# A two-layer encoder on one core: shorter decay chain, middle conv taps on ScalarE, rotary products beside the root, keys and queries transposed later

## The chip, the cores and the metric

The kernel runs on one core of a Trainium2 chip. The metric is the device time of one execution in microseconds, the median of several runs. TensorE (PE) multiplies matrices into PSUM banks, VectorE (DVE), ScalarE (ACT) and GpSimd (POOL) do the elementwise work, SyncE (SP) issues most DMA loads.

## The reference

The input is x (1, 256, 1024). After a LayerNorm, two layers each add a token mixer and a mixture of 32 experts, and normalise again:

```
p = h @ w_in                                   # 1024 -> 5648
ya = attention(rope(rms(aq)), rope(rms(ak)), av)          # 8 heads, 2 kv heads
yb = neighbourhood attention(bq, bk, bv) + rpb            # 4 heads
q, k, v = silu(conv5(cq, ck, cv)); q, k = l2norm(q), l2norm(k)
beta = sigmoid(b); g = -exp(A_log) * softplus(a + dt_bias)
yc = rms(delta_forward + delta_backward) * silu(cz)       # chunks of 64
mix = sig(ga)*(ya @ wa) + sig(gb)*(yb @ wb) + sig(gc)*(yc @ wc)
h = LN(alpha*h + mix @ w_out);  h = LN(alpha*h + moe(h))
```

In the delta rule g is summed within a chunk and exponentiated (the decay), beta weighs the update, and each chunk needs the inverse of a unit triangular 64x64 matrix per head.

## The kernel before

All 256 tokens stand in two tiles of 128 partitions (t = 0, 1). A layer is a mixer (about 0 to 235 us, and 705 to 940) and a MoE stage whose expert weights stream in.

**The mixer's projections** are the main line. The weights come in units in the order of ORDER (ga0, cqk, cz, cv, akv, aq, ga1, bqk, bv, gb, gc), then the branch weights and w_out. For each unit SP loads w, ACT casts the high part uh, and DVE or (indices of POOL) GpSimd subtracts it to get the low part ul (`stream`, L278); PE then makes three products, high by high, low by high, high by low (`mm3`, L192). Loads run four units ahead. Where places of the mixer come free, loads of expert weights are issued between them (`fetch_freed`, L406).

**Side lines** are generators: "delta" (`delta_line`, L625), "key" (L599), "query" (L611) and "attention" (L1013, L1050). `pump` (L339) steps a line between projection matmuls once an estimated PE clock has passed its due time, and LAGS (L47) holds the lag after each yield. So LAGS sets where a side line's PE work stands among the projections. PE's order is the written one (`pinned`); the orders of DVE, ACT, POOL and SP are made by a scheduler from the program and its priorities.

**Delta line.** cz has beta's and the decay's raw inputs in columns 256 to 272. They are copied to ba (L630); from them come beta (tanh) and g, by a series for softplus on 16 columns, ten scalar_tensor_tensor steps (L174 is `stt`, L169 and L171 are `ts` with one and two scalars, L165 is `tt`). g and its two halves feed eb, six small matmuls into a PSUM bank; db spreads g for the pairwise decays E, which POOL and DVE mask and multiply by beta. qk is the transposition to token-major of the convolved q and k (cs0, cs1), followed by a square, a sum and the root (`rsqrt`, L239: DVE scales and adds eps, POOL takes the power -0.5), kh and qd are the normalised products, kT, qdT their transpositions, gr the grams. Out of them comes the inverse: a round trip through DRAM, some thirty small POOL steps, two writes to DRAM, and two loads back on SP (placeC<-d).

**Conv** (L554): per channel half a first tap on DVE (128x256, `ts`) and four more by `stt`.

**Keys and queries** (`norm_rope`, L569): square on ACT, sum and scale on DVE, root on POOL, product with the root on DVE, two rotary products on POOL, product with the cosine and the sum on DVE. kTA and qTA are their transpositions on PE.

**Merge** (L1123): each branch's product is weighted by its gate and summed into mix; `turn_mix` transposes mix (tpm).

In the trace, "placeA" to "placeK" are the mixer's places of SBUF, "gap" a small one (g, ba, beta's and decay's tiles), "sb" and "eb" PSUM banks.

Of the kernel before, what the change touches and what calls it, by code (L numbers as in the profile page):

```python
# [48 lines left out]
    "key": [10.0],  # L49
    "query": [16.22, 1.92, 1.92],  # L50
# [67 lines left out]
def kernel(ctx: ExitStack, tc: tile.TileContext, a: dict, out: bass.AP):  # L118
# [120 lines left out]
    def rsqrt(o, x, scale, eps, n):  # L239

        with tc.high_priority(offset=PRI):
            ts(V, o, x, scale, OP.mult, eps, OP.add)
            return G.tensor_tensor(out=o, in0=o, in1=mhalf[:, :n], op=OP.pow)
# [74 lines left out]
    def mixer(l, fetch, norm):  # L318
# [233 lines left out]
        cs = [of(f"cs{i}", 2, S) for i in range(3)]  # L552

        def conv(i, b):  # L554

            bv = b.rearrange("p (m s) -> p m s", m=2)
            y = of(f"cy{i % 2}", 2, S)
            for m in range(2):
                ch = 2 * i + m
                ts(V, y[:, m], bv[:, m], cw[:, ch, 2:3], OP.mult)  # L560
                for j in (0, 1, 3, 4):
                    s = j - 2
                    t0, t1 = max(0, -s), S - max(0, s)
                    stt(y[:, m, t0:t1], bv[:, m, t0 + s:t1 + s], cw[:, ch, j:j + 1], y[:, m, t0:t1],
                        OP.mult, OP.add)
            A.activation(bv, y, AF.Tanh)
            stt(cs[i], bv, 1.0, y, OP.add, OP.mult)


        def norm_rope(b, t, n, which, dst, name):  # L570
# [3 lines left out]
            xv = x8(x[:, :n * 64])  # L574
            raw = x8(b) if which else xv
            if not which:
                A.copy(x[:, :n * 64], b)
            sq = y
            A.activation(sq[:, :n * 64], b if which else x[:, :n * 64], AF.Square)
            rs = of(f"rs{t}", 8)  # L580
            V.tensor_reduce(out=rs[:, :n], in_=x8(sq[:, :n * 64]), axis=AX.X, op=OP.add)
            rsqrt(rs[:, :n], rs[:, :n], 1.0 / 64.0, 1e-6, n)
            tt(V, xv, raw, rs[:, :n, None].to_broadcast([128, n, 64]), OP.mult)
            yv = x8(y[:, :n * 64])
            s5 = gc_[:, which, 1, t].rearrange("p (a b e) -> p a b e", a=2, b=2)
            for b_ in range(2):
# [38 lines left out]
        def delta_line(vbank, zb):  # L625

            szg = of("szg", 2, 256)
            ba = of("ba", 2, 2, 2, 4)
            for t in range(2):
                V.tensor_copy(ba[:, :, :, t], zb[t][:, 256:272].rearrange("p (a d h) -> p a d h", a=2, d=2))  # L630
                A.activation(szg[:, t], zb[t][:, :256], AF.Tanh, scale=0.5)
                stt(szg[:, t], szg[:, t], 1.0, zb[t][:, :256], OP.add, OP.mult)
            tt(G, szg.rearrange("p t (h d) -> p (t h) d", d=64), szg.rearrange("p t (h d) -> p (t h) d", d=64),
               gn[:, 2:3].to_broadcast([128, 8, 64]), OP.mult)
# [4 lines left out]
            av = ba[:, 1].rearrange("p d t h -> p (d t h)")  # L639
# [3 lines left out]

            def dh(ap8):

                return ap8.rearrange("p (d h) -> p d h", d=2)[:, :, None, :].to_broadcast([128, 2, 2, 4])

            xx, ax, ee, ss, pp, g = (sc[:, i] for i in range(6))

            sb = bank("s", f"sb{l}")  # L650
            rr, sq_, acc = (sb[:, 16 * i:16 * i + 16] for i in range(3))
            tt(V, xx.rearrange("p (d t h) -> p d t h", d=2, t=2), ba[:, 1], dh(al[:, 1]), OP.add)
# [5 lines left out]
            tt(V, ss, ee, rr, OP.mult)  # L658
            tt(V, pp, sq_, ss, OP.mult)
# [32 lines left out]
            edl = ev[:, 16:32].rearrange("p (d x) -> p d x", d=2)  # L692
# [25 lines left out]
            for t in range(2):  # L718
# [8 lines left out]
                rsqrt(rk[:, t], rk[:, t], 1.0, 1e-6, 8)  # L727
# [35 lines left out]
            G.tensor_copy(kq[:, 1], cs[0])  # L763
# [359 lines left out]
        def merge(br):  # L1123
# [545 lines left out]
```

## Time and profile before

| what | us |
|---|---|
| median of 3 runs | 1431.82 |
| lowest, highest | 1430.55, 1435.36 |
| profiled execution, own time | 1430.76 |
| its span | 1429.0 |
| mean granted clock of TensorE | 0.986 |

The span is what the views show; the execution's own time is 1.76 us more. A row of a timeline has the start, the duration, the engine and line, the instruction (out<-in) with its shape, and in brackets how long the engine stood idle before it and what released it. Rows of the same instruction in sequence are drawn together (x8). A row of windows gives for a stretch the time that PE was busy and the mean clock granted to it, 1.00 being 2.4 GHz.

### The profile page before, as it was taken

How to read it: one execution, taken by the hardware profiler on the slowest of the kernel's cores; microseconds unless marked ns; L12 is line 12 of the kernel's file. 1: busy time of each engine (PE TensorE's matmuls, PEld its weight loads, DVE VectorE, ACT ScalarE, POOL GpSimd, SP SyncE). 2: the span in 40 equal slices, each digit the busy share in tenths (PEclk: the TensorE clock that was granted, in tenths of full speed). 3: DMA queues.
4: the chain of work that ended last, by engine and by line, in shares of the span. 5: the costliest groups of instructions: out<-in, count | busy, mean ns of one | idle time of the engine just before them, and what ended most of it. 6: DMA issues, size and time to landing. Idle time of an engine off the chain costs nothing. (4 is left out here: it accounts for less than half of the span.)

```text
span 1429.0 us, 23895 instructions
## 1 busy us (share of the span) xinstructions
PE 1347.2 (94%) x9778; PEld 893.0 (62%) x9778; DVE 610.5 (43%) x1221; ACT 400.2 (28%) x761; POOL 257.9 (18%) x327
## 2 busy tenths in 40 slices
PE   8999999899999999999889999999999899999986
PEld 7877787655555555554477877875565555655632
DVE  6887567522221222222368866773222122222214
ACT  4445543221111111111145465332111111111111
POOL 4475303300000000000046661132000000000000
PEclk9989999999999999999999999999999999999998
DMA  7635769899999999999856466798999999999994
GB/s 233 211 118 142 257 235 356 312 407 419 419 419 417 419 419 420 418 419 420 334 154 195 123 195 228 271 352 322 419 419 418 418 419 418 420 419 419 418 419 194
DMA packets 114531, 479.86 MB, mean 336 GB/s; under 512 B 25168, under 2 KB 38000, under 8 KB 65520
## 3 DMA queue, kind: packets, MB, share of 16 engines
q1 hardware_dynamic: 112464, 471.85, 84.6%
q0 software_dynamic: 1376, 5.24, 1.0%
q8 instruction: 79, 1.29, 0.4%
q10 hardware_dynamic: 576, 1.18, 0.2%
q14 instruction: 36, 0.29, 0.1%
HBM read 476.40 MB, written 1.84 MB: 335 GB/s over the span
## 5 line engine op out<-in xcount | busy, mean ns | idle before, releaser
L180 PE MATMUL h<-w,h 128*64 128x256 f32 x2016 | 231.3, 385 | 19.4 <-PEq L1413 9.5
L180 PEld LDWEIGHTS h<-w,h 128*64 128x64 f32 x2016 | 143.5, 138 | 98.1 <-issue 14.9
L174 DVE SCALAR_TENSOR_TENSOR hid<-gate,h 128x256 f32<-128x256 f32 x64 | 26.9, 421 | 395.1 <-ACT gate L1505 395.1
L174 DVE SCALAR_TENSOR_TENSOR op<-mo,rt,op 64x512 fp32r<-64x512 f32 x128 | 96.0, 750 | 221.8 <-ACT op L1536 220.9
L1536 ACT ACTIVATE op<-mo,rt 64x512 fp32r<-64x512 f32 x128 | 87.4, 683 | 311.2 <-PE mo L180 271.7
L180 PE MATMUL mo<-w,hidT 128*64 128x512 f32 x720 | 167.7, 595 | 3.6 <-ACT hidT L1517 1.4
L165 POOL TENSOR_TENSOR W<-P,rt 128x128 f32<-128x128 f32 x64 | 24.2, 398 | 773.2 <-PE PT L186 700.9
L1505 ACT ACTIVATE gate<-h 128x256 f32<-128x256 f32 x64 | 24.5, 383 | 404.3 <-PE h L180 404.3
L180 PEld LDWEIGHTS mo<-w,hidT 128*64 128x64 f32 x720 | 51.3, 137 | 92.2 <-issue 79.3
L180 PE MATMUL h<-w,xg 128*64 128x256 f32 x864 | 96.9, 380 | 2.4 <-ACT h L1479 2.4
L180 PE MATMUL h<-wl,h 128*64 128x256 f32 x768 | 86.3, 381 | 2.2 <-ACT h L1479 1.4
L180 PEld LDWEIGHTS h<-w,xg 128*64 128x64 f32 x864 | 61.0, 137 | 34.3 <-ACT h L1479 3.8
L180 PEld LDWEIGHTS h<-wl,h 128*64 128x64 f32 x768 | 53.9, 137 | 30.6 <-ACT h L1479 2.4
L180 PE MATMUL mo<-wl,hidT 128*64 128x512 f32 x304 | 70.0, 597 | 1.6 <-DMA wl<-in_w_dram 1.5
L180 PE MATMUL my<-op,PT 128*128 128x512 f32 x256 | 69.3, 410 | 0.8 <-DVE op L174 0.6
L180 PEld LDWEIGHTS my<-op,PT 128*128 128x128 f32 x256 | 45.4, 188 | 23.9 <-issue 13.2
L180 PE MATMUL xg<-P,hh 128*128 128x256 f32 x256 | 54.8, 294 | 0.0
L180 PEld LDWEIGHTS xg<-P,hh 128*128 128x128 f32 x256 | 39.1, 188 | 24.5 <-issue 24.2
L180 PE MATMUL h<-wl,xg 128*64 128x256 f32 x416 | 48.3, 382 | 5.5 <-DMA wl<-in_w_dram 3.9
L180 PE MATMUL xg<-P,hl 128*128 128x256 f32 x256 | 51.1, 281 | 0.0
L180 PEld LDWEIGHTS mo<-wl,hidT 128*64 128x64 f32 x304 | 20.6, 137 | 36.5 <-issue 30.1
L180 PEld LDWEIGHTS h<-wl,xg 128*64 128x64 f32 x416 | 28.6, 137 | 23.0 <-DMA wl<-in_w_dram 7.1
(458 smaller groups left out, 2451.1 us busy)
## 6 DMA issues: line engine op xcount, KB each, us to landing
w<-in_w_dram SPq DMA_DIRECT2D x268, 1024.0 KB, 19.9
wl<-in_w_dram SPq DMA_DIRECT2D x112, 1024.0 KB, 19.9
w_gb<-in_w_in_dram SPq DMA_DIRECT2D x16, 512.0 KB, 3.5
w_gc<-in_w_in_dram SPq DMA_DIRECT2D x16, 512.0 KB, 4.5
w_wo<-in_w_out_dram SPq DMA_DIRECT2D x16, 512.0 KB, 4.4
w_ga<-in_w_in_dram SPq DMA_DIRECT2D x14, 512.0 KB, 5.7
w_cqk<-in_w_in_dram SPq DMA_DIRECT2D x8, 512.0 KB, 3.4
w_aq<-in_w_in_dram SPq DMA_DIRECT2D x8, 512.0 KB, 4.8
```

The lines of the kernel that those rows point to most:

```text
L165: return eng.tensor_tensor(out=o, in0=x, in1=y, op=op).ins
L174: return V.scalar_tensor_tensor(out=o, in0=x, scalar=s, in1=y, op0=op0, op1=op1)
L180: ins = T.matmul(o, l, r, start=start, stop=stop, skip_group_check=True).ins
L1505: A.activation(g, b[:, :256], AF.Tanh, scale=0.5)
L1536: A.activation(hi, src, AF.Copy, scale=w)
```

## The change

Seven edits. (1) LAGS: the key line steps 15 instead of 10 after its start, the query line 22.5 instead of 16.22. (2) The middle tap of each conv half is an activation on ACT. (3) cs0 is an alias of kq[:, 1], so the copy L763 goes. (4) In `norm_rope` the rotary and cosine products take the unscaled input, the root is multiplied in last; keys work in place in PSUM; the scale and eps of the roots of keys, queries and qk are on POOL. (5) The decay chain reads cz's bank instead of ba, has -exp(A_log) ready as nea, keeps more operands in PSUM, and writes the two halves of g straight from acc; beta and the szg product come later. (6) A second exponential of eb stays in PSUM and feeds nbe and kds. (7) Branch c's merge writes into its PSUM bank and sums into mix on DVE at high priority.

```diff
-    "key": [10.0],
-    "query": [16.22, 1.92, 1.92],
+    "key": [15.0],
+    "query": [22.5, 1.92, 1.92],
...
-    def rsqrt(o, x, scale, eps, n):
+    def rsqrt(o, x, scale, eps, n, eng=V):
...
-            ts(V, o, x, scale, OP.mult, eps, OP.add)
+            ts(eng, o, x, scale, OP.mult, eps, OP.add)
...
-        cs = [of(f"cs{i}", 2, S) for i in range(3)]
+        cs = [kq[:, 1]] + [of(f"cs{i}", 2, S) for i in (1, 2)]
...
-                ts(V, y[:, m], bv[:, m], cw[:, ch, 2:3], OP.mult)
+                A.activation(y[:, m], bv[:, m], AF.Copy, scale=cw[:, ch, 2:3])
...
-            if not which:
-                A.copy(x[:, :n * 64], b)
-            sq = y
-            A.activation(sq[:, :n * 64], b if which else x[:, :n * 64], AF.Square)
+            A.copy(x[:, :n * 64], b)
+            A.activation(dst, x8(b) if which else xv, AF.Square)
...
-            rsqrt(rs[:, :n], rs[:, :n], 1.0 / 64.0, 1e-6, n)
-            tt(V, xv, raw, rs[:, :n, None].to_broadcast([128, n, 64]), OP.mult)
+            rsqrt(rs[:, :n], rs[:, :n], 1.0 / 64.0, 1e-6, n, G)
...
+            xv = x8(b) if which else xv
             tt(V, xv, xv, gc_[:, which, 0, t:t + 1].to_broadcast([128, n, 64]), OP.mult)
-            tt(V, dst, xv, yv, OP.add)
+            tt(V, xv, xv, yv, OP.add)
+            tt(V, dst, xv, rs[:, :n, None].to_broadcast([128, n, 64]), OP.mult)
...
-            for t in range(2):
-                V.tensor_copy(ba[:, :, :, t], zb[t][:, 256:272].rearrange("p (a d h) -> p a d h", a=2, d=2))
...
-            A.activation(beta, ba[:, 0].rearrange("p d t h -> p d (t h)"), AF.Tanh, scale=0.5)
-            ts(V, beta, beta, 0.5, OP.mult, 0.5, OP.add)
...
+            for t in range(2):
+                tt(V, by_t(xx)[:, :, t], by_d(zb[t][:, 264:272]), by_d(al[:, 1]), OP.add)
+            for t in range(2):
+                A.activation(by_t(th_)[:, :, t], by_d(zb[t][:, 256:264]), AF.Tanh, scale=0.5)
...
-            ts(V, xx, xx, 0.0, OP.max)
-            stt(acc, acc, 2.0, xx, OP.mult, OP.add)
-            tt(V, g.rearrange("p (d t h) -> p d t h", d=2, t=2), acc.rearrange("p (d t h) -> p d t h", d=2, t=2),
-               dh(ea), OP.mult)
-            ts(V, g, g, -1.0, OP.mult)
+            stt(acc, xx, 0.0, acc, OP.max, OP.add)
+            tt(V, g, acc, nea, OP.mult)
+            for c2 in range(2):
+                decayed = stt(sc[:, c2], acc, C("half")[:, c2:c2 + 1], nea, OP.mult, OP.mult).ins
...
+            ts(V, beta, th_, 0.5, OP.mult, 0.5, OP.add)
...
-                ts(V, sc[:, c2], g, C("half")[:, c2:c2 + 1], OP.mult)
...
+            A.activation(eb[:, 64:128], eb[:, :64], AF.Exp)
             A.activation(ev, eb[:, :64], AF.Exp)
...
-                rsqrt(rk[:, t], rk[:, t], 1.0, 1e-6, 8)
+                rsqrt(rk[:, t], rk[:, t], 1.0, 1e-6, 8, G)
...
-            G.tensor_copy(kq[:, 1], cs[0])
...
-                    stt(x, x, 1.0, b, OP.add, OP.mult)
-                    if br != "a":
-                        tt(G if br == "b" or t else V, mix[:, t, sl], mix[:, t, sl], x, OP.add)
+                    if br != "c":
+                        stt(x, x, 1.0, b, OP.add, OP.mult)
+                        if br == "b":
+                            tt(G, mix[:, t, sl], mix[:, t, sl], x, OP.add)
+                    else:
+                        with tc.high_priority(offset=PRI):
+                            stt(b, x, 1.0, b, OP.add, OP.mult)
+                            tt(V, mix[:, t, sl], mix[:, t, sl], b, OP.add)
```

What this moves in the built program stands at three places. The first is DVE at the end of the decay chain, before eb (g and its halves are in gap, the accumulator in sb). Before:

```order
L174 SCALAR_TENSOR_TENSOR sb_606<-sb_606,gap_83 128x16
L190 TENSOR_TENSOR ul_ga_868<-w_ga_767,uh_ga_867 128x1024
L165 TENSOR_TENSOR gap_83<-sb_606,gap_83 128x16
L581 TENSOR_REDUCE placeS_108<-placeH_105 128x2
L169 TENSOR_SCALAR gap_83<-gap_83 128x16
L171 TENSOR_SCALAR placeS_108<-placeS_108 128x2
L169 TENSOR_SCALAR gap_83<-gap_83,placeK_109 128x16 x2
```

And now:

```order
L174 SCALAR_TENSOR_TENSOR sb_596<-sb_596,gap_83 128x16
L174 SCALAR_TENSOR_TENSOR placeA_99<-cv_513,placeS_108,placeA_99 128x254
L174 SCALAR_TENSOR_TENSOR sb_596<-gap_83,sb_596 128x16
L174 SCALAR_TENSOR_TENSOR placeA_99<-cv_513,placeS_108,placeA_99 128x255
L165 TENSOR_TENSOR gap_83<-sb_596,gap_83 128x16
L174 SCALAR_TENSOR_TENSOR gap_83<-sb_596,placeK_109,gap_83 128x16
L190 TENSOR_TENSOR ul_ga_774<-w_ga_711,uh_ga_773 128x1024
L174 SCALAR_TENSOR_TENSOR gap_83<-sb_596,placeK_109,gap_83 128x16
L171 TENSOR_SCALAR placeS_108<-sb_596 128x16
```

What were four instructions for g and its halves are three, without the sign flip; the first cut of ga1 (ul_ga) stands behind g instead of three of them ahead, and the taps of cv (placeA<-cv) are still under way.

The second is PE at the first transposition of the queries, among bqk's products. Before:

```order
L180 MATMUL bqk_982<-placeT_110,ul_bqk_962 128x256
L186 MATMUL qdT_1038<-cst,placeF_103 128x128 x4
L186 MATMUL qdT_1044<-cst,placeF_103 128x128 x4
L186 MATMUL qTA_1050<-cst,placeE_102 128x128 x4
L180 MATMUL bqk_981<-placeT_110,uh_bqk_961 128x256
```

And now:

```order
L180 MATMUL bqk_985<-placeT_110,uh_bqk_988 128x256
L180 MATMUL bqk_985<-placeU_111,uh_bqk_988 128x256
L180 MATMUL bqk_985<-placeT_110,ul_bqk_989 128x256
L180 MATMUL bqk_985<-placeT_110,uh_bqk_988 128x256
L180 MATMUL bqk_985<-placeU_111,uh_bqk_988 128x256
L180 MATMUL bqk_985<-placeT_110,ul_bqk_989 128x256
L186 MATMUL qTA_1177<-cst,placeE_102 128x128 x4
```

qTA stood right behind qdT, inside the second unit of bqk; now twelve products, the sixteen grams and twelve more products lie between. In the same way kTA, which stood between db and the last aq products, now stands behind three products of ga1, and all six last aq products come before the qk transpositions.

The third is POOL behind the decays E (placeF) and DVE at the first unit of bqk. On POOL (placeH<-placeH,placeA is a rotary product, mhalf the power of a root, placeD<-placeA a kd product), before:

```order
L165 TENSOR_TENSOR placeF_103<-placeF_103,placeK_109 128x512
L165 TENSOR_TENSOR placeF_103<-placeF_103,placeS_108 128x512
L243 TENSOR_TENSOR placeS_108<-placeS_108,mhalf 128x8 x3
L165 TENSOR_TENSOR placeH_105<-placeH_105,placeA_99 128x16x16 x2
L243 TENSOR_TENSOR placeS_108<-placeS_108,mhalf 128x8
L165 TENSOR_TENSOR placeH_105<-placeH_105,placeA_99 128x16x16 x2
```

And now:

```order
L165 TENSOR_TENSOR placeH_105<-placeH_105,placeA_99 128x16x16 x2
L165 TENSOR_TENSOR placeF_103<-placeF_103,placeK_109 128x512
L165 TENSOR_TENSOR placeF_103<-placeF_103,placeS_108 128x512
L171 TENSOR_SCALAR placeS_108<-placeS_108 128x8
L243 TENSOR_TENSOR placeS_108<-placeS_108,mhalf 128x8
L171 TENSOR_SCALAR placeS_108<-placeS_108 128x8
L165 TENSOR_TENSOR placeH_105<-placeH_105,placeA_99 128x16x16
L243 TENSOR_TENSOR placeS_108<-placeS_108,mhalf 128x8
L165 TENSOR_TENSOR placeH_105<-placeH_105,placeA_99 128x16x16
L171 TENSOR_SCALAR placeS_108<-placeS_108 128x8
L243 TENSOR_TENSOR placeS_108<-placeS_108,mhalf 128x8
L165 TENSOR_TENSOR placeD_101<-placeA_99,placeS_108 128x512 x2
```

The rotary products of the first query tile stand ahead of the mask and beta products of E, those of the second between the roots, and each root has its TENSOR_SCALAR on POOL. On DVE, at ul_bqk (placeA<-qk is kh, placeF<-qk are qd), before:

```order
L165 TENSOR_TENSOR placeA_99<-qk_835,placeS_108 128x256
L165 TENSOR_TENSOR placeF_103<-qk_835,gap_83 128x256 x2
L190 TENSOR_TENSOR ul_bqk_944<-w_bqk_865,uh_bqk_943 128x1024
L165 TENSOR_TENSOR placeA_99<-qk_847,placeS_108 128x256
L165 TENSOR_TENSOR placeF_103<-qk_847,gap_83 128x256 x2
```

And now:

```order
L165 TENSOR_TENSOR placeA_99<-qk_835,placeS_108 128x256
L165 TENSOR_TENSOR placeF_103<-qk_835,gap_83 128x256 x2
L165 TENSOR_TENSOR placeA_99<-qk_847,placeS_108 128x256
L190 TENSOR_TENSOR ul_bqk_947<-w_bqk_862,uh_bqk_946 128x1024
L165 TENSOR_TENSOR placeF_103<-qk_847,gap_83 128x256 x2
```

ul_bqk has changed places with kh of the second tile. Later, SP issues the first load of gc behind the two loads of the inverse instead of ahead of them; ACT's cast of that unit stands before the exponentials of the third attention step instead of behind them; and six more gb products stand on PE before that step's transposition.

## Rows read from the trace of the kernel before

**Rows 1.** The page, part 1: busy us, share, instructions of PE; PEld, DVE, ACT, POOL.
```profile
PE 1347.2 (94%) x9778; PEld 893.0 (62%) x9778; DVE 610.5 (43%) x1221; ACT 400.2 (28%) x761; POOL 257.9 (18%) x327
```

**Rows 2.** Timeline of PE, both mixers: start, duration, instruction [idle before <-releaser].
```profile
71.02 1.23 PE L180 MATMUL eb<-gap,placeK 128*128 128x8 f32 x8 [3.14 <-DVE gap L169]
...
101.17 0.44 PE L186 MATMUL qTA<-cst,placeE 128*128 128x128 f32 x2 [2.73 <-DVE placeE L165]
...
121.14 0.33 PE L186 MATMUL pT_a<-cst,placeH 128*128 128x128 f32 x1 [0.59 <-DVE placeH L169]
...
775.06 2.74 PE L180 MATMUL eb<-gap,placeK 128*128 128x8 f32 x12 [3.38 <-DVE gap L169]
...
806.03 0.69 PE L186 MATMUL qTA<-cst,placeE 128*128 128x128 f32 x2 [3.52 <-DVE placeE L165]
```

**Rows 3.** Windows of PE: stretch, us, PE busy, granted clock, DMA share, GB/s.
```profile
70.00:80.00 10.00, 8.98 (x29) 0.66 0.44 135
100.00:110.00 10.00, 8.83 (x84) 0.83 0.54 173
770.00:785.00 15.00, 11.62 (x44) 0.77 0.48 150
805.00:815.00 10.00, 8.97 (x87) 0.83 0.52 164
```

**Rows 4.** Timeline of DVE in the first mixer.
```profile
53.03 0.47 DVE L169 TENSOR_SCALAR placeA<-cv,placeS 128x256 f32<-128x256 f32 x1
...
61.98 0.16 DVE L169 TENSOR_SCALAR sb<-gap 128x16 f32<-128x16 f32 x1
...
62.35 1.23 DVE L171 TENSOR_SCALAR placeS<-placeS 128x2 f32<-128x2 f32 x1
...
64.92 1.21 DVE L190 TENSOR_TENSOR ul_ga<-w_ga,uh_ga 128x1024 fp32r<-128x1024 f32 x1
...
109.72 1.31 DVE L190 TENSOR_TENSOR ul_bv<-w_bv,uh_bv 128x512 fp32r<-128x512 f32 x1 [0.94 <-ACT uh_bv L190]
```

**Rows 5.** Timeline of ACT in the first mixer.
```profile
82.75 0.60 ACT L577 COPY placeH<-aq 128x512 f32<-128x512 f32 x1
...
139.12 0.47 ACT L992 ACTIVATE placeH<-s_a,placeS 128x256 f32<-128x256 f32 x1 [2.15 <-PE o_a L180]
...
145.06 1.05 ACT L190 CAST uh_gc<-w_gc 128x1024 fp32r<-128x1024 f32 x1 [2.81 <-DMA w_gc<-in_w_in_dram]
```

**Rows 6.** Timeline of POOL, first mixer and (last row) second.
```profile
27.52 0.31 POOL L169 TENSOR_SCALAR placeS<-placeS 128x30 f32<-128x30 f32 x1 [6.53 <-DMA placeS<-in_conv_w_dram]
...
80.19 1.79 POOL L165 TENSOR_TENSOR placeF<-placeF,placeK 128x512 f32<-128x512 f32 x1 [2.40 <-DVE placeF L165]
82.06 1.04 POOL L165 TENSOR_TENSOR placeF<-placeF,placeS 128x512 f32<-128x512 f32 x1
83.21 5.48 POOL L243 TENSOR_TENSOR placeS<-placeS,mhalf 128x8 f32<-128x8 f32 x3
89.56 2.42 POOL L165 TENSOR_TENSOR placeH<-placeH,placeA 128x256 f32<-128x256 f32 x2 [0.87 <-DVE placeH L165]
...
787.06 6.47 POOL L243 TENSOR_TENSOR placeS<-placeS,mhalf 128x8 f32<-128x8 f32 x3
```

**Rows 7.** Timeline of PE, first mixer, from the first qk transposition on.
```profile
79.58 0.38 PE L186 MATMUL qk<-cst,placeB 128*128 128x128 f32 x2
...
80.38 0.48 PE L180 MATMUL aq<-uh_aq,placeT 128*128 128x512 f32 x1
...
81.15 0.40 PE L180 MATMUL ga<-uh_ga,placeT 128*128 128x512 f32 x1
...
92.67 0.28 PE L180 MATMUL bqk<-placeU,uh_bqk 128*128 128x256 f32 x1
92.78 0.28 PE L180 MATMUL bqk<-placeT,ul_bqk 128*128 128x256 f32 x1
...
145.87 1.03 PE L186 MATMUL pT_a<-cst,placeH 128*128 128x128 f32 x8
```

More of the change, by code (lines that the diff above doesn't have):

```diff
@@ L573, in norm_rope @@
             x, y = of(f"ring{turn}", 512), of(f"ring{turn + 1}", 512)
-            xv = x8(x[:, :n * 64])
-            raw = x8(b) if which else xv
-            if not which:
-                A.copy(x[:, :n * 64], b)
-            sq = y
-            A.activation(sq[:, :n * 64], b if which else x[:, :n * 64], AF.Square)
+            xv, yv = x8(x[:, :n * 64]), x8(y[:, :n * 64])
+            A.copy(x[:, :n * 64], b)
+            A.activation(dst, x8(b) if which else xv, AF.Square)
             rs = of(f"rs{t}", 8)
-            V.tensor_reduce(out=rs[:, :n], in_=x8(sq[:, :n * 64]), axis=AX.X, op=OP.add)
-            rsqrt(rs[:, :n], rs[:, :n], 1.0 / 64.0, 1e-6, n)
-            tt(V, xv, raw, rs[:, :n, None].to_broadcast([128, n, 64]), OP.mult)
-            yv = x8(y[:, :n * 64])
+            V.tensor_reduce(out=rs[:, :n], in_=dst, axis=AX.X, op=OP.add)
+            rsqrt(rs[:, :n], rs[:, :n], 1.0 / 64.0, 1e-6, n, G)
             s5 = gc_[:, which, 1, t].rearrange("p (a b e) -> p a b e", a=2, b=2)
@@ L627, in delta_line @@
             szg = of("szg", 2, 256)
-            ba = of("ba", 2, 2, 2, 4)
-            for t in range(2):
-                V.tensor_copy(ba[:, :, :, t], zb[t][:, 256:272].rearrange("p (a d h) -> p a d h", a=2, d=2))
[L631 to L634, printed above, removed]
+            sb = bank("s", f"sb{l}")
+            rr, sq_, acc, th_ = (sb[:, 16 * i:16 * i + 16] for i in range(4))
+            by_t = lambda ap: ap.rearrange("p (d t h) -> p d t h", d=2, t=2)
+            by_d = lambda ap: ap.rearrange("p (d h) -> p d h", d=2)
             beta = of("beta", 2, 8)
-            A.activation(beta, ba[:, 0].rearrange("p d t h -> p d (t h)"), AF.Tanh, scale=0.5)
-            ts(V, beta, beta, 0.5, OP.mult, 0.5, OP.add)
             sc = of("gsc", 8, 16)
-            av = ba[:, 1].rearrange("p d t h -> p (d t h)")
+            xx, ax, ee, ss, pp, g = (sc[:, i] for i in range(6))
             ea = of("ea", 8)
@@ L642, in delta_line @@
                 A.activation(ea, al[:, 0], AF.Exp)
[L644 to L652, printed above, removed]
+            nea = sc[:, 6]
+            for t in range(2):
+                ts(G, by_t(nea)[:, :, t], by_d(ea), -1.0, OP.mult)
+            for t in range(2):
+                tt(V, by_t(xx)[:, :, t], by_d(zb[t][:, 264:272]), by_d(al[:, 1]), OP.add)
+            for t in range(2):
+                A.activation(by_t(th_)[:, :, t], by_d(zb[t][:, 256:264]), AF.Tanh, scale=0.5)
+                A.activation(szg[:, t], zb[t][:, :256], AF.Tanh, scale=0.5)
+                stt(szg[:, t], szg[:, t], 1.0, zb[t][:, :256], OP.add, OP.mult)
             stt(ax, xx, -1.0, xx, OP.mult, OP.max)
@@ L657, in delta_line @@
             tt(V, sq_, ee, rr, OP.mult)
-            tt(V, ss, ee, rr, OP.mult)
-            tt(V, pp, sq_, ss, OP.mult)
+            stt(ss, ee, 2.0, rr, OP.mult, OP.mult)
+            stt(pp, sq_, 0.5, ss, OP.mult, OP.mult)
             ts(V, acc, pp, 1.0 / 19.0, OP.mult)
@@ L686, in delta_line @@
             for c2 in range(2):
-                ts(V, sc[:, c2], g, C("half")[:, c2:c2 + 1], OP.mult)
                 mm(eb[:, 32 + c2 * 16:48 + c2 * 16], C("ones"), sc[:, c2], True, True)
             ev = of("ev", 64)
+            A.activation(eb[:, 64:128], eb[:, :64], AF.Exp)
             A.activation(ev, eb[:, :64], AF.Exp)
             egc = ev[:, 0:16].rearrange("p (d x) -> p d x", d=2)
-            edl = ev[:, 16:32].rearrange("p (d x) -> p d x", d=2)
+            egp, edl = (eb[:, 64 + 16 * i:80 + 16 * i].rearrange("p (d x) -> p d x", d=2) for i in range(2))
             egl = ev[:, 32:64].rearrange("p (c d t h) -> p c d t h", c=2, d=2, t=2)
@@ L697, in delta_line @@
                 t, hs = c // 2, slice(c % 2 * 64, c % 2 * 64 + 64)
-                stt(nbe[hs, c], egc[hs, 0, t * 4:t * 4 + 4], -1.0, beta[hs, 0, t * 4:t * 4 + 4], OP.mult, OP.mult)
-                ts(V, nbe[hs, 3 - c], egc[hs, 1, t * 4:t * 4 + 4], -1.0, OP.mult)
+                stt(nbe[hs, c], egp[hs, 0, t * 4:t * 4 + 4], -1.0, beta[hs, 0, t * 4:t * 4 + 4], OP.mult, OP.mult)
+                ts(V, nbe[hs, 3 - c], egp[hs, 1, t * 4:t * 4 + 4], -1.0, OP.mult)
             kds = of("kds", 2, 8)
```

2 lines of the change are left out of this document (added).

## The prediction

> **What bounds the kernel now.** I read the page's busy shares first: TensorE (PE) is busy for 94% of the span [rows 1], so time can be won only where it stands still or runs slowly. PE's order is written out and fixed, so the second view is PE's timeline, for its waits. Each mixer holds two long ones [rows 2]: the decay sums eb wait for DVE, 3.14 us in the first layer and 3.38 in the second, and the queries' transposition qTA waits for DVE's last product, 2.73 and 3.52. Together that is 12.77 us. A short wait stands before the first softmax's transposition, 0.59. Third come the windows: behind each of the four long waits the granted clock falls towards its lower level, 1.2 of 2.4 GHz [rows 3]. A mean of 0.66 over 10 us is a loss of 3.4 us; the other three rows give 1.7, 0.23 x 15 = 3.45, and 1.7. Sum 10.25. So the change can remove 12.77 + 10.25 = **23.0 us**, if both waits vanish and nothing takes their place.
>
> **The change, part by part.**
>
> *The decay wait (conv taps, decay chain, roots).* PE is through with what it has at 71.02 - 3.14 = 67.9 and waits for g. DVE works without a gap ahead of it, so what counts is how much DVE work still stands there. Six taps of 0.47 go to ScalarE [rows 4]: 2.8. A TENSOR_SCALAR that writes SBUF takes 1.23 while POOL works, one that writes PSUM 0.16 [rows 4]; three such held ones go (operands in PSUM, the root's scale on POOL): 3.2. Three ul_ga of 1.21 [rows 4], ahead of g so far, stand behind it now: 3.6. The last taps of cv and the second half of the key's norm go behind it as well. Together 9.6 us, against the 3.1 needed; were half of that wrong, 4.8 would still do. What is late next is ACT (its taps and the key's square), for which some 1.7 us are left. I take the wait and the low clock behind it as gone.
>
> *The queries' wait.* Both qTA now stand behind the grams. The second query root ends on POOL after the third one of the next paragraph: two kd products of at most 1.79 each, a scale and a root of 1.83, together some 5.6 us [rows 6]. PE has 60 bqk matmuls at 0.11 from start to start [rows 7] and 28 smaller ones between there and the first qTA, over 8 us, and DVE's last product of 0.7 fits as well. The wait goes.
>
> *The new wait: bqk's first lo part.* PE cannot pass its third bqk matmul without ul_bqk. On DVE that subtraction used to stand before the second kh product; now it stands behind it, and this product waits for POOL's third root. Ahead of the root POOL has the rotary products, which used to come after. From the last aq matmul I add: query copy 0.60 [rows 5]; rotary pair 2.42; mask product 1.79; beta product 1.04; three roots 5.48; second rotary pair 2.42 [rows 6]; three scales of 128x8, each put at 0.2, between nothing and the 0.31 of one with 30 columns [rows 6], 0.6; kh, by the tap of its size, 0.47 [rows 4]; ul_bqk 1.21, by ul_ga's shape. Sum 16.0. PE over the same stretch: from the first qk transposition to the third bqk matmul 92.78 - 79.58 = 13.20, less 0.77 for three aq (80.38 to 81.15), and with the four key transpositions that now lie in it, at half of the 0.80 that eight of qk take: 12.8 [rows 7]. So PE waits **3.2 us per layer**. Bounds: 1.3 (copy beside the first bank's end, scales free, the mask product at the beta product's 1.04) and 4.5 (the roots at the second layer's 6.47, scales at 0.31). Behind waits of 2.73 to 3.52 the low level cost 1.7 or more [rows 2, 3], and 3.2 lies among these. But PE was at full clock and busy for long before this place, so it may also pass; I charge 1.7 once for the two layers (bounds 0 and 3.4).
>
> The scales on POOL are the place where a rule speaks against the change. The rows have 0.31 us for a scale on POOL and 1.23 for a held one on DVE [rows 4, 6]. The Trainium skill (GPSIMD Engine Reference, 4.1 Engine selection) sends elementwise work to VectorE and calls POOL about twice as slow on two inputs. By that each scale would cost twice DVE's unheld 0.16, and the wait would be 0.4 us longer per layer, an estimate; by the rows DVE is the dearer place as long as POOL holds it up. The sum stands without this.
>
> *The third attention step.* ACT's cast of the first w_gc stood behind that step's exponentials; now it stands before them. SP used to issue that load ahead of the two loads of the inverse, and now issues it behind them. The load that stood behind them before landed at 145.06 [rows 5]. The chain that leads there starts with the grams on DVE, where a wait of 0.94 for a cast [rows 4] need not come again: 144.1. Then a cast of 1.05, four exponentials of 0.47 [rows 5], and three short steps (the o_a cast, two on DVE) at the tap's 0.47: ready at 148.4. PE's transposition stood at 145.87 [rows 7]. Six more gb matmuls stand before it, 1.5 by the three aq, and the 0.59 is gone: 146.8. So it waits 1.6 us (bounds 0, and 2.5 with the 0.94 kept), against 0.59 that goes: net **1.0 per layer**.
>
> *What costs nothing.* The alias of cs0 takes a copy off POOL at a time when POOL then waits for DVE; without that cover it would be a gain. The merge's last sums on DVE spare the tail's transpositions a wait for POOL, and the later transposition of yc gives about as much back. The beta tanh, beta and nea lie beside other work. In the MoE stage the loads start when mixer places come free, so what the mixer gains passes through.
>
> *Sum.* 23.0 - 6.4 - 1.7 - 2.0 = 12.9 us. The profiled execution took 1430.76 (span 1429.0), 1.06 under the median of the three runs shown. 1430.76 - 12.9 = 1417.9; on the median's footing **1418.9**. Its own range by the bounds: 23.0 - 2.6 + 1.2 = 21.6 gained, 1410.2, up to 23.0 - 9.0 - 1.7 - 3.8 = 8.5 gained, 1423.3.
>
> **The rivals.**
>
> *No new wait at bqk.* It needs 3.2 us less ahead of ul_bqk, and the third step as before: all of 23.0 is kept, 1408.8. For it: POOL's spans are rough, and a root that DVE does not hold up may be shorter. Against it: 5.48 and 6.47 for three roots. Chance 0.20.
>
> *All new waits at their upper bounds.* 4.5 + 1.7 + 1.9 per layer, 16.2 in all, so 6.8 are left: 1425.0. For it: the second layer's rows are the longer ones. Chance 0.16.
>
> *Slower: the inverse's loads do not come earlier with PE.* Place: SP holds w_gc behind those loads, ACT stands in its cast before the exponentials, PE waits before the third transposition. If that load lands at 145.06 as before, the transposition is ready at 145.06 + 1.05 + 1.9 + 1.4 = 149.4 instead of 145.87, 3.5 later in each layer whatever was won ahead, and the low level costs 1.7 on top: 1431.8 + 10.4 = 1442.2. It decides once those loads move by less than 3.5 us. Against it: the grams that start the chain come earlier by as much as PE does. Chance 0.07.
>
> *The change does not do what it says.* eb still waits, now for ACT's taps and the key's square, or what the mixer wins is waited for again at the MoE's loads: 1431.8. Against it: 9.6 us of DVE work moved for 3.1 us of wait. Chance 0.07.
>
> **How the numbers follow.** The forecast has 0.50. The range 1408 to 1425 holds it with its bounds, the rival without a wait, and the near half of the one with all waits; outside lie the other half, the slower rival and the idle one, some 0.2. A measurement here can tell about 0.3% from no change, 4.3 us. Faster by more: the forecast, the first rival and nearly all of the second, with a little off for waits not seen, 0.80. Within it: the idle rival and that rest, 0.12. Slower: 0.08.
>
> **What would show it.** Right: neither eb nor qTA among PE's waits, a wait of bqk for ul_bqk of 2 to 4 us, one of pT_a near 1.6 in the third step, the clock at 1.00 through the decay matmuls. Wrong: eb still waits for DVE or for ACT; the low level comes without a wait ahead of it; the third step waits over 3 us; or no wait stands at bqk and the time is near 1409.

## The result, and the profile after

The changed kernel is **slower**: a median of 1442.3 us over 7 runs (1436.96 to 1446.8) against 1431.38 for the kernel before over 7 runs beside it (1428.9 to 1435.36). The ratio is 1.0067, with a 95% interval of 1.005 to 1.0084. The forecast was 1418.9, the range 1408 to 1425. The profiled execution has the lowest time of the seven: 1436.96, span 1435.3, mean clock 0.987. So the trace below shows 6.2 us of loss (1436.96 - 1430.76) where the medians show 10.9. One execution of an experiment below (both repairs) took 2701.29 us: its median of 1442.75 includes that one, its ratio does not.

The page, part 1, answers to [rows 1]:

```profile
PE 1349.2 (94%) x9778; PEld 894.8 (62%) x9778; DVE 596.6 (42%) x1195; ACT 405.1 (28%) x781; POOL 250.4 (17%) x337
```

DVE lost 13.9 us of work, ACT gained 4.9, POOL lost 7.5, as the edits say. PE is still busy for 94%, and again its waits decide. The timeline of PE after, the answers to [rows 2] (start, duration, instruction, idle before it and who ended it):

```profile
91.56 0.58 PE L180 MATMUL bqk<-placeT,ul_bqk 128*128 128x256 f32 x1 [3.40 <-DVE ul_bqk L190]
...
120.22 0.55 PE L186 MATMUL pT_a<-cst,placeH 128*128 128x128 f32 x3 [0.65 <-DVE placeH L169]
...
147.53 0.72 PE L186 MATMUL pT_a<-cst,placeH 128*128 128x128 f32 x4 [2.44 <-DVE placeH L169]
148.44 0.76 PE L186 MATMUL pT_a<-cst,placeH 128*128 128x128 f32 x4 [0.19 <-DVE placeH L169]
...
176.01 0.24 PE L180 MATMUL L<-placeC,placeF 32*32 32x32 f32 x2 [1.46 <-ACT placeC L860]
...
223.29 0.50 PE L180 MATMUL y0b<-uh_br0b,ym 128*128 128x512 f32 x1 [1.06 <-DVE mix L174]
...
798.88 0.58 PE L180 MATMUL bqk<-placeT,ul_bqk 128*128 128x256 f32 x1 [3.43 <-DVE ul_bqk L190]
...
854.79 0.72 PE L186 MATMUL pT_a<-cst,placeH 128*128 128x128 f32 x4 [2.39 <-DVE placeH L169]
```

The two long waits of before, eb and qTA, are gone in both layers. In their place stand one at bqk (3.40 and 3.43) and one at the third attention step (2.44 and 2.39). New, too, are L (1.46, with 0.36 right behind it) and y0b. The windows of PE after (stretch, us, PE busy, granted clock, DMA share, GB/s), the answers to [rows 3]:

```profile
70.00:80.00 10.00, 8.67 (x40) 1.00 0.47 146
90.00:100.00 10.00, 8.44 (x48) 0.66 0.28 77
100.00:110.00 10.00, 10.00 (x108) 1.00 0.54 175
140.00:150.00 10.00, 7.37 (x34) 0.95 0.65 230
150.00:160.00 10.00, 10.00 (x100) 0.88 0.68 212
...
770.00:785.00 15.00, 14.51 (x71) 1.00 0.65 202
...
790.00:800.00 10.00, 6.57 (x31) 0.88 0.43 159
800.00:810.00 10.00, 10.00 (x92) 0.78 0.34 101
805.00:815.00 10.00, 10.00 (x110) 1.00 0.48 159
...
850.00:860.00 10.00, 7.42 (x30) 0.83 0.54 183
```

The low level did not go, it moved. Behind the bqk waits it costs 0.34 x 10 = 3.4 us in the first layer and (0.12 + 0.22) x 10 = 3.4 in the second; behind the third step's 0.5 + 1.2 = 1.7 and again 1.7. That is 10.2 us, as much as the 10.25 of before.

**Where the time goes along the mixer.** I took the start of the same PE instructions in both traces. In the first layer the changed kernel leads by 4.78 us at the first bqk product, 2.78 at the first gb, and it trails by 4.65 at the last pT_a, 5.39 at the last o_b and 5.35 at the first tpm. At the first tp of the second layer it trails by 4.76: the MoE stage hands the mixer's shift on. So the loss arises between the bqk products and the merge.

### The profile page after: what moved, and what is told of

Read it like the earlier page. It is cut to its first block, busy times and chain, and to the rows that moved or that the text cites. A ratio compares the mean times of both kernels' runs of the same rounds, so it can differ in the third digit from the quotient of the medians.

```text
span 1435.3 us, 23921 instructions
## 1 busy us (share of the span) xinstructions
PE 1349.2 (94%) x9778; PEld 894.8 (62%) x9778; DVE 596.6 (42%) x1195; ACT 405.1 (28%) x781; POOL 250.4 (17%) x337
## 3 DMA queue, kind: packets, MB, share of 16 engines
HBM read 476.40 MB, written 1.84 MB: 333 GB/s over the span
```

## The experiments

Behind each median stand, in brackets, its ratio to the kernel before, timed beside it, and the 95% interval of that ratio. The first question was which of the two new waits, or which edit, carries the loss.

**The root's scale back on DVE** (only for qk; the keys' and queries' roots stay on POOL):

```diff
-                rsqrt(rk[:, t], rk[:, t], 1.0, 1e-6, 8, G)
+                rsqrt(rk[:, t], rk[:, t], 1.0, 1e-6, 8)
```

> The changed kernel with one call put back: the scale and eps of the qk roots on DVE again. In the built order the first ul_bqk then stands ahead of the second kh product. Theory (the time went into the waits at bqk and at the third attention step and into the low clock behind each): the wait of bqk for ul_bqk falls from 3.4 to about 1 us or less in each layer and the low clock behind it (3.4 us) goes with it, some 5 us per layer: about 1432 against the 1442.3 of the changed kernel; the third step still waits 2.4. Rival (the moved transpositions or the PSUM operands cost the time by themselves): less than 3 us change.

Measured: 1439.43 (1.0054, 1.0039 to 1.0068). The bqk wait falls to 1.82 and the clock behind it to 0.83 instead of 0.66 (1.7 us instead of 3.4), and PE leads by 7.66 us at the last bqk product. At the last pT_a it trails the kernel before by 4.27 all the same, the changed kernel by 4.65. Of the 3.64 won on the changed kernel up to bqk's end, 0.71 is left behind the first attention step, whose transposition waits in this run by

```profile
118.15 0.30 PE L186 MATMUL pT_a<-cst,placeH 128*128 128x128 f32 x1 [0.82 <-POOL placeJ L165]
119.49 0.55 PE L186 MATMUL pT_a<-cst,placeH 128*128 128x128 f32 x3 [1.04 <-DVE placeH L169]
```

where the changed kernel waits 0.65 (a gb product waits 0.72 before them); 0.4 is left behind the third step, whose wait has grown to 2.78. The expected 1432 was missed.

**The inverse's loads on POOL's queue**, so that SP is free for w_gc:

```diff
-                SP.dma_start(Wc[:, w], d2[w].rearrange("x p j -> p x j"))
+                for hf in (0, 8):
+                    G.dma_start(Wc[:, w, hf:hf + 8], d2[w, hf:hf + 8].rearrange("x p j -> p x j"))
```

> The changed kernel with the two loads of the inverse issued by POOL (in four halves) instead of SP, so that the first gc weight load is not queued behind them. Theory: the third attention step's wait (2.4 and 0.2 us per layer) goes, and the low clock behind it (1.7): some 4 us per layer, about 1434; bqk still waits 3.4 us. Rival (the wait has another cause than the load's place on SP, for instance the cast's place on ACT alone): the wait stays at 2 us or more, the time within 2 us of the changed kernel.

Measured: 1440.06 (1.0054, 1.0041 to 1.0068). The third step's long wait is gone, but PE now waits for POOL at T, 1.96 us in the first layer and 5.00 in the second, and the expected 1434 was missed. The timeline of POOL shows why ("issue" is a wait for nothing that the profile shows):

```profile
136.06 0.93 POOL L818 DMA_DIRECT2D placeC<-d  x1 [1.22 <-DMA d<-placeB]
139.66 0.91 POOL L818 DMA_DIRECT2D placeC<-d  x1 [2.68 <-issue]
142.99 0.88 POOL L818 DMA_DIRECT2D placeC<-d  x1 [2.42 <-issue]
146.44 0.89 POOL L818 DMA_DIRECT2D placeC<-d  x1 [2.57 <-issue]
```

Issuing four loads took POOL 11.3 us; SP issues the two of the changed kernel in 1.48. The cure brought a cost of its own.

**Both, with the queries' rotary products ordered behind their own root:**

```diff
-                rsqrt(rk[:, t], rk[:, t], 1.0, 1e-6, 8, G)
+                rsqrt(rk[:, t], rk[:, t], 1.0, 1e-6, 8)
...
-            rsqrt(rs[:, :n], rs[:, :n], 1.0 / 64.0, 1e-6, n, G)
+            root = rsqrt(rs[:, :n], rs[:, :n], 1.0 / 64.0, 1e-6, n, G)
...
-                tt(G, o, i0, i1, OP.mult)
+                with ExitStack() if which else tc.issue_after(root.ins):
+                    tt(G, o, i0, i1, OP.mult)
...
-                SP.dma_start(Wc[:, w], d2[w].rearrange("x p j -> p x j"))
+                for hf in (0, 8):
+                    G.dma_start(Wc[:, w, hf:hf + 8], d2[w, hf:hf + 8].rearrange("x p j -> p x j"))
```

> The changed kernel with both repairs (qk scale on DVE, loads of the inverse on POOL) and the queries' rotary products ordered behind their own root on POOL. Theory: both new waits and the low clock behind them go, some 10 us per layer off the changed kernel: 1420 to 1424, faster than before. Rival (the time lies elsewhere): above 1432.

Measured: 1442.75 (1.007, 1.0057 to 1.0084). bqk waits only 0.83, but qTA waits 2.95 again, T 1.55 and in the second layer 5.25, L and y0b as in the changed kernel. Missed: curing single waits did not bring the time down, so I turned to the edit that sets PE's order.

**The lags alone, on the kernel before:**

```diff
-    "key": [10.0],
-    "query": [16.22, 1.92, 1.92],
+    "key": [15.0],
+    "query": [22.5, 1.92, 1.92],
```

> The kernel before with only the two numbers of LAGS changed. Theory: the queries' wait goes (2.7 and 3.5 us and 1.7 of low clock each), eb's wait stays, and the third attention step's wait comes with the move of the order on SP and ACT (about 2.6 us and 1.7 of low clock per layer): within 4 us of before, no wait at bqk. Rival (the third step's wait comes from the other edits): no wait there, about 1422.

Measured: 1446.75 (1.0099, 1.0078 to 1.0119), some 15 us slower than before, where I expected no more than 4. The timeline of PE in this run:

```profile
70.99 1.77 PE L180 MATMUL eb<-gap,placeK 128*128 128x8 f32 x12 [3.05 <-DVE gap L169]
...
104.37 0.90 PE L186 MATMUL qTA<-cst,placeE 128*128 128x128 f32 x3 [3.32 <-DVE placeE L165]
...
149.99 0.72 PE L186 MATMUL pT_a<-cst,placeH 128*128 128x128 f32 x4 [2.56 <-DVE placeH L169]
...
178.47 0.24 PE L180 MATMUL L<-placeC,placeF 32*32 32x32 f32 x2 [1.47 <-ACT placeC L866]
...
225.74 0.50 PE L180 MATMUL y0b<-uh_br0b,ym 128*128 128x512 f32 x1 [1.07 <-DVE mix L174]
```

Without any other edit the lags bring the waits at the third step, L and y0b, and they do not even take away the one at qTA, for which I had credited them.

**The changed kernel with the lags as before:**

```diff
-    "key": [15.0],
-    "query": [22.5, 1.92, 1.92],
+    "key": [10.0],
+    "query": [16.22, 1.92, 1.92],
```

> The changed kernel with the two numbers of LAGS as before. Theory (the later queries shift the attention line and the delta line against the projections, and this alone costs the waits at the third step, at L, ks, y0b and y0c and the low clock behind them; the other edits gain): PE's order is that of the kernel before, so those waits are gone; eb does not wait (a gain of 6.5 us per layer); the bqk wait of about 3 us may stay: 1420 to 1427, faster than before. Rival (the other edits lose by themselves): not faster than before.

Measured: **1420.42** (1418.7 to 1422.73), 0.9922 (0.9909 to 0.9935): faster than both kernels. A hit. PE's timeline has no wait at eb, bqk, L or y0b, and none over 0.6 at pT_a; what is left of note is

```profile
74.00 0.55 PE L186 MATMUL kTA<-cst,placeG 128*128 128x128 f32 x3 [2.00 <-ACT placeG L601]
...
96.31 0.76 PE L186 MATMUL qTA<-cst,placeE 128*128 128x128 f32 x3 [2.05 <-DVE placeE L165]
```

From bqk to the first tpm PE leads the kernel before by a steady 4 to 5 us; at the end of the second layer by 10.5. The other six edits together are worth about 11 us.

**Only the key's lag changed** (query back to 16.22, key at 15):

```diff
-    "query": [22.5, 1.92, 1.92],
+    "query": [16.22, 1.92, 1.92],
```

> The changed kernel with the queries' lag back at 16.22 and the keys' at 15. Theory (it is the queries' lag that shifts the attention line): as with both numbers back, within 3 us of it. Rival (the keys' lag does the harm): within 3 us of the changed kernel, 1439 to 1445.

Measured: 1422.98 (0.994, 0.9927 to 0.9953). A hit: the key's lag costs about 2.6 us, so the query's, set on top of it, costs 1442.3 - 1423.0 = 19.3. The wait at bqk stands here in full (3.40 and 3.42), and yet the kernel is fast: in the kernel with the old lags waits at kTA and qTA stand in its place. SP's timeline shows what the query's lag turns round:

```profile
124.97 0.37 SPq L286 DMA_DIRECT2D w_gc<-in_w_in_dram  x1
137.32 1.67 SPq L817 DMA_DIRECT2D placeC<-d  x2
139.10 9.02 SPq L286 DMA_DIRECT2D w_gc<-in_w_in_dram  x6
```

Here the first w_gc is issued at 124.97, ahead of the inverse's loads. Even though those come 2.3 us later than in the changed kernel (134.99, below), the third step waits for nothing.

**The middle taps back on DVE, lags as before:**

```diff
-                A.activation(y[:, m], bv[:, m], AF.Copy, scale=cw[:, ch, 2:3])
+                ts(V, y[:, m], bv[:, m], cw[:, ch, 2:3], OP.mult)
```

> The changed kernel with LAGS as before and the middle conv taps on DVE again. Theory (the taps are a small part of the DVE work that left): g is still ready before PE, 2.8 us of DVE work ahead of it more, so within 2 us of the version without the taps put back. Rival (the taps decide): eb waits 2 us or more again and the time is 4 us or more above it.

Measured: 1421.25 (0.9929, 0.9916 to 0.9943). As expected, the taps don't decide: the kTA wait grows to 0.62 + 3.35, the qTA wait goes. The eb wait stays away without the 2.8 us that I had counted for them.

**The inverse's loads on ACT's queue:**

```diff
-                SP.dma_start(Wc[:, w], d2[w].rearrange("x p j -> p x j"))
+                A.dma_start(Wc[:, w], d2[w].rearrange("x p j -> p x j"))
```

> The changed kernel with one place altered: the inverse's two loads are issued on ScalarE's queue instead of SyncE's, so the load of the first gc unit no longer stands behind them on SP; PE's order is as in the changed kernel. If the single place (w_gc behind the inverse's loads, cast before the exponentials) carries the cost, the wait of pT_a near 147.5 (2.4 us in each layer) and the low clock behind it go and the time falls to 1430 or less. If the cost is spread over PE's later order, the wait goes but others (L, the neighbour steps) take its place: 1436 to 1443, as with the loads on POOL.

Measured: 1453.58 (1.015, 1.0134 to 1.0166), outside both expectations. The timeline of ACT:

```profile
133.78 1.69 ACTq L817 DMA_DIRECT2D placeC<-d  x2
135.59 1.04 ACT L190 CAST uh_gb<-w_gb 128x1024 fp32r<-128x1024 f32 x1 [13.58 <-issue]
```

ACT stood for 13.58 us in front of a load whose data was not written yet, and PE waited 7.45 for the gate behind it. The run says nothing on the third step; it gives the price of putting a load that is not yet free to go on ACT's queue here.

**A query lag in between:**

```diff
-    "query": [22.5, 1.92, 1.92],
+    "query": [19.0, 0.8, 1.92],
```

with the key's at 10.

> The changed kernel with key lag 10 as before and query lags 19.0, 0.8, 1.92, between before's 16.22 and the change's 22.5. SP again issues the first gc load behind the inverse's loads, but ACT's cast of it stands behind most exponentials of the third step. If SP's order costs, a third-step wait returns and the time is 1426 or more; if what costs is how far attention and delta steps fall back against the projections, this small step costs under 3 us: 1418 to 1424.

Measured: 1427.73 (0.9969, 0.9958 to 0.9981), 7.3 us over the one with the lags as before. By the time the first theory holds, by the trace neither: SP has w_gc behind the inverse's loads (131.72, then 133.29), but no wait stands at the third step, since ACT's cast is behind most of its exponentials. PE waits 2.23 at the first pT_a (0.59 with the lags as before), 1.01 at y0a (0.41) and 1.32 at tpm (0.95), while the wait of qTA is gone. So each shift of that number makes a new set of waits, and SP's order alone does not make the third step's.

**Two tries at a better kernel**, with the lags as before: the sum of squares of the norms at high priority, and the qk scale on DVE.

```diff
-            V.tensor_reduce(out=rs[:, :n], in_=dst, axis=AX.X, op=OP.add)
+            with tc.high_priority(offset=PRI):
+                V.tensor_reduce(out=rs[:, :n], in_=dst, axis=AX.X, op=OP.add)
```

> The changed kernel with the lags as before, and the sum of squares of the norms at high priority on DVE, which puts the query roots ahead of the inverse's kd products on POOL. If the qTA wait of 2.0 us (with its low clock) is set by those roots, it shrinks below 1 us and the time is 1414 to 1418; if DVE's last products set it, the time stays within 2 us of 1420.4.

Measured: 1431.13 (0.9996, 0.9985 to 1.0007). Missed: kT now waits 1.68 and bqk 1.42, and qTA 2.34 still. The second one is the edit of the first experiment, on the kernel with the old lags.

> The changed kernel with the lags as before and the scale and eps of the qk roots on DVE, as before, instead of POOL. If the scale on POOL is the cheaper place, kh and what follows come later and the time rises by 2 to 4 us (1422 to 1425); if POOL's roots are what counts, as at the new wait for ul_bqk, it falls to 1416 to 1419; if the place is covered here, it stays within 2 us of 1420.4.

Measured: 1421.9 (0.9928, 0.9914 to 0.9943), 1.5 above the one with the scale on POOL: the place is covered there.

**The first gc unit on ACT's queue**, the lags as in the change. This load is free to go when ACT comes to it, and the orders of PE, DVE and POOL are the changed kernel's:

```diff
-            SP.dma_start(w, src)
+            (A if "gc0" in name and "gc0" not in srcs[len(loaded) - 1][1] else SP).dma_start(w, src)
```

> The changed kernel with one DMA moved: the first gc unit of each layer is issued on ScalarE's queue behind the second attention step's copies, instead of on SyncE behind the inverse's loads; the orders of PE, DVE and POOL are those of the changed kernel. If SP's holding of that load sets the third step's wait, the cast and the subtraction that stand ahead of the step's row maxima come early, the pT_a wait of 2.4 us and the low clock behind it go in both layers, and the time falls by 6 to 9 us, to 1433 to 1436; the waits of L and y0b (1.8 and 1.1 us a layer) stay, since the inverse's own chain is not touched. If those waits hang on the inverse alone and take up what is won, PE only waits longer at L, by up to what it comes earlier, and the time stays within 3 us of 1442.

Measured: **1434.77** (1.0021, 1.0013 to 1.003), 7.5 us under the changed kernel. A hit for the first theory. First the chain in the changed kernel, by the timelines of SP, ACT and DVE:

```profile
134.99 1.48 SPq L817 DMA_DIRECT2D placeC<-d  x2
136.56 13.74 SPq L286 DMA_DIRECT2D w_gc<-in_w_in_dram  x6
```

```profile
141.78 1.05 ACT L190 CAST uh_gc<-w_gc 128x1024 fp32r<-128x1024 f32 x1 [7.40 <-DMA w_gc<-in_w_in_dram]
```

```profile
142.86 1.23 DVE L190 TENSOR_TENSOR ul_gc<-w_gc,uh_gc 128x1024 fp32r<-128x1024 f32 x1 [8.91 <-ACT uh_gc L190]
144.01 1.28 DVE L983 TENSOR_REDUCE placeS<-s_a 128x2 f32<-128x512 f32 x2
145.21 0.55 DVE L169 TENSOR_SCALAR placeS<-placeS 128x2 f32<-128x2 f32 x2
```

Then the same with the load on ACT, by the timelines of ACT and DVE and the windows of PE:

```profile
121.76 0.39 ACTq L286 DMA_DIRECT2D w_gc<-in_w_in_dram  x1
...
135.14 1.05 ACT L190 CAST uh_gc<-w_gc 128x1024 fp32r<-128x1024 f32 x1 [0.74 <-PE gb L180]
```

```profile
136.22 1.23 DVE L190 TENSOR_TENSOR ul_gc<-w_gc,uh_gc 128x1024 fp32r<-128x1024 f32 x1 [2.30 <-ACT uh_gc L190]
137.36 1.28 DVE L983 TENSOR_REDUCE placeS<-s_a 128x2 f32<-128x512 f32 x2
```

```profile
140.00:150.00 10.00, 10.00 (x53) 1.00 0.83 285
150.00:160.00 10.00, 10.00 (x160) 1.00 0.65 211
```

The step's row maxima on DVE stand behind ul_gc, that behind ACT's cast, that behind the load, and the load on SP behind the inverse's. With the load issued at 121.76 instead of 136.56, the maxima start at 137.36 instead of 144.01, and the wait of pT_a and its low clock are gone in both layers. The waits at L (1.48), y0b (1.07) and bqk (3.44) stand as they did; that of L did not grow, though PE comes there 4.7 us earlier. So the second theory falls.

The two traces, however, lie only 1.8 us apart (1435.12 against 1436.96), where the medians have 7.5. In the first layer PE leads by 1.42 at the last bqk product, by nothing behind the first attention step (its transposition waits 0.81 and 1.04 in this run), by 4.75 at the first T, and by 3.20 from o_b on. In the second layer the four leads are 2.65, 0.04, 4.63 and 3.07. So the third step wins 4.8 and 4.6, some 1.5 a layer is given back right behind L, and what the first layer had won is lost again at the second layer's first attention step, where the clock is 0.83 from 820 to 830 in this trace and 1.00 in that of the changed kernel. At L, too, the clock falls in this run, by the windows

```profile
170.00:180.00 10.00, 8.33 (x112) 0.83 0.57 188
...
875.00:885.00 10.00, 8.16 (x93) 0.83 0.64 244
```

while in the trace of the changed kernel it stays at 1.00 behind the same waits. The 7.5 us are the measurement; that the changed kernel mostly loses more than in the execution of the trace is only seen in the mean clocks: 0.987 to 0.992 with its three lowest times (1436.96 to 1438.38), 0.981 to 0.985 with the four others (1442.3 to 1446.8). By PE's 1349 us of work, 0.005 of clock is an estimated 6.7 us.

## Why the prediction was wrong

**Right:** the removals. eb and qTA wait no more (12.77 us), and the low clock of [rows 3] is at 1.00 in the same places. Without the lags the eb wait stays away as well, with the taps on either engine; but that qTA stands behind the grams is not reason enough for its wait to go: it stays at 3.32 when the lags are moved by themselves.

**Right:** the new wait at bqk, forecast 3.2 a layer, measured 3.40 and 3.43, and by the mechanism named. POOL and DVE after, the answers to [rows 6]:

```profile
76.39 2.42 POOL L165 TENSOR_TENSOR placeH<-placeH,placeA 128x256 f32<-128x256 f32 x2 [0.28 <-ACT placeH L575]
...
82.58 0.20 POOL L171 TENSOR_SCALAR placeS<-placeS 128x8 f32<-128x8 f32 x1
82.86 1.66 POOL L243 TENSOR_TENSOR placeS<-placeS,mhalf 128x8 f32<-128x8 f32 x1
...
88.28 1.64 POOL L243 TENSOR_TENSOR placeS<-placeS,mhalf 128x8 f32<-128x8 f32 x1
```

```profile
89.95 0.42 DVE L165 TENSOR_TENSOR placeA<-qk,placeS 128x256 f32<-128x256 f32 x1 [1.61 <-POOL placeS L243]
90.30 1.22 DVE L190 TENSOR_TENSOR ul_bqk<-w_bqk,uh_bqk 128x1024 fp32r<-128x1024 f32 x1
```

From the first rotary product to the end of ul_bqk the prediction had 16.0 - 0.6 = 15.4 us; it took 91.52 - 76.39 = 15.13. A scale on POOL takes 0.20, the value taken. That the wait itself came so near is partly luck, for two errors cancel. The copy of the queries started at 75.71 only, behind ACT's copies of db, so from the first qk transposition (74.01) to the end of ul_bqk it took 17.5 us and not 16.0; and PE came to its third bqk product after 91.56 - 3.40 - 74.01 = 14.1 us and not 12.8, 0.78 of that a wait of qk. The Trainium skill (GPSIMD Engine Reference, 4.1 Engine selection) sends elementwise work to VectorE. Its factor of about two is for two inputs; a scale reads one tensor, which the section calls roughly line-rate on POOL, so the 0.4 us of the prediction did not follow from it. At this place the run agrees with sending it to VectorE: with the scale on DVE, where it took 0.16 and 0.17, the bqk wait fell from 3.40 to 1.82, though a held one took DVE 1.23 before [rows 4]. The order changed with it, however: ul_bqk then stood ahead of the second kh product. With the old lags the two places differ by 1.5 us, which no measurement here can tell from nothing.

**Wrong:** the sizes. Both layers, us of the profiled execution:

| term | forecast | measured |
|---|---|---|
| waits and low clock removed | -23.0 | -23.0 |
| bqk wait | 6.4 | 6.8 |
| low clock behind it | 1.7 | 6.8 |
| third step: longest wait and its low clock, against the short waits of before | 2.0 | 9.1 |
| db (0.55) and qk (0.78, 0.49) | 0 | 1.8 |
| L, 1.82 a layer, less 0.33 and 0.34 of before at T | 0 | 3.0 |
| merge: y0b, y0c against y0a, tpm | 0 | -1.3 |
| sum | -12.9 | +3.2 |

Third step: (2.44 + 0.19) + (2.39 + 0.19) + 3.4, plus 0.48 by which the first pT_a waits longer. Merge: 1.06 + 0.40 + 1.06 + 0.39, less 0.42 + 0.41 and two times 0.94 + 0.73. The profiled execution lost 6.2. Of the 3.0 that the table does not hold, 2.2 are short waits that the kernel before did not have, in each layer 0.5 in three waits at ks and 0.6 in three at tpm; 0.8 are not assigned. The median lost 4.7 more than this execution, the lowest of the seven; of that there is no trace, only the lower clocks told above.

**The step that failed** is "*The third attention step*", net 1.0 per layer, and it failed in three of its terms. It let ACT's cast be followed by exponentials and "three short steps" of 0.47. In truth ul_gc (1.23), two maxima (1.28 together) and two scales (0.55) stand on DVE between cast and exponentials: from the cast's start to pT_a it took 147.53 - 141.78 = 5.75, not 4.35. It let the 0.59 go, but that wait stands at the first attention step, and it stayed, at 0.65 and 1.00. And it charged no low clock, which came to 1.7 a layer behind a wait of 2.4. Of the 7.1 us between the 2.0 and the 9.1 of the table, 3.4 are the clock, 2.0 the longer wait and 1.7 the wait that did not go. The 0.94 that it granted is not among the errors: the cast started 145.06 - 141.78 = 3.3 us earlier, while PE came to the transposition at 147.53 - 2.44 = 145.1, 1.7 before the 146.8 of the forecast, so the chain won 1.6 on PE. The run with the load on ACT's queue gives a price of 7.5 us for both layers by the medians; in the traces the step wins 4.8 and 4.6, of which some 1.5 a layer go again behind L.

**The low clock at bqk** was "1.7 once for the two layers (bounds 0 and 3.4)"; in this execution it was 3.4 in each. With the key's lag alone the same wait of 3.40 cost 1.7 (0.83 in the window from 90 to 100), as it did with the load on ACT. So the price of one wait was in the bounds, but it fell due in both layers, and the 0.66 of eb's window [rows 3], behind a wait of 3.14, would have been the upper bound.

**The lags as an edit.** The forecast treated the later transposition as a free cure for one wait plus three named places. The runs show that it is the edit that costs: 19.3 us for the query's number, 15 for both lags on the kernel before. Of the 19.3 the two traces hold 10.2 (1436.96 against 1426.80, the highest of five with the key's lag alone). In the first layer they part by 7.6 us between the qk transpositions and the first tpm, and these rows come to 7.5 (the other waits there nearly cancel, 2.9 against 3.4): the third step's waits 2.63 and its low clock 1.7, low clock behind bqk 3.4 instead of 1.7, and 1.5 at L (1.82 against 0.34 at T). The other 9.1 are the spread of executions, 3.8 on the one side and 5.3 on the other. What L waits for is in the timeline of ACT in the changed kernel:

```profile
174.45 1.03 ACT L190 CAST uh_gc<-w_gc 128x1024 fp32r<-128x1024 f32 x1
175.38 1.17 ACT L860 COPY placeC<-T 32x512 f32<-32x512 f32 x2
```

T is done at 172.28, but its copies stand behind four exponentials of the neighbourhood step (172.46 to 174.36) and this cast. With the query lag of 19 they stand behind two of the four exponentials, and L does not wait. That this order on ACT is the cause is read from the traces alone; no run moved the copies.

**The rivals.** "Slower: the inverse's loads do not come earlier with PE" had named place, chain and 1442.2 us, and was given 0.07. The chain is the one that the last run shows, and the time is that of the median, but the latter is partly chance: its price held 3.5 + 1.7 a layer for the third step and kept nothing of what was won ahead, where the trace has 2.6 + 1.7 there, a gain ahead, and losses at bqk and L that it did not hold. Its bound "less than 3.5 us" was too sharp as well: the loads moved by 3.6, and the wait came. Against it I had set that the grams move with PE; they did, but the work between load and transposition was longer than I had it.

**Pass-through** of the mixer's shift to the MoE stage was right: 5.35 at the first tpm, 4.76 at the next layer's start. With the old lags it is 4.6 and 2.7, but there the clock from 420 to 440 is 0.83 against 0.91 in the kernel before, 1.6 of the 1.9 us; so it is not shown that a gain passes less fully than a loss.

## What to carry to other kernels

A number that sets where one line stands among others is not one edit: it reorders every queue behind it, so weigh it by itself, before it is taken together with edits that gain. When a load moves behind another on its queue, follow it to the first instruction that PE waits for, through every engine in between and all that stands ahead of the step there (here cast, subtraction, maxima, exponentials), and charge the low clock behind the wait. And where waits stand in a row, curing the first is worth little until the next is cured: the root's scale on DVE put PE 7.66 us ahead at the end of bqk instead of 4.02, and of these 3.64 the first attention step left 0.71 and the third step 0.4.

## What the runs showed of the hardware

Between two of the four loads on POOL's queue stood 2.4 to 2.7 us in the first layer and 2.7 to 3.2 in the second, in which POOL did nothing else; on SP two larger ones took 1.48 together. A load on ACT's queue that was not free to go held ACT for 13.58 us; one that was cost it 0.39. And the low level does not follow from the length of a wait alone. Behind 3.4 us at bqk it cost 3.4 us in one trace and 1.7 in two others; behind 1.84 at L 1.7 in the run with the load on ACT and nothing in the changed kernel, where 0.88 had stood in the window from 150 to 160; behind 2.05 at qTA 1.7 with the old lags, and behind 2.00 at kTA in the same trace nothing; at the third step, with the scale on DVE, 1.7 behind 2.78 in the first layer and nothing behind 2.61 in the second. In these traces a wait of 1.8 to 3.4 us thus cost anything from nothing to 3.4 us of clock, and of the two kernels the one with more of them also scatters more: 9.8 us between its executions, against 4.0 with the old lags.
